# Cross-attention stage of a decoder layer: row factor in the softmax's scale, memory squares from a second load, a buffer per key result, sample scores in half pairs

## The chip, the core and the metric

The kernel runs on one core of a Trainium2 chip. The metric is device time in microseconds (us) of one execution, the median over several runs. The engines are PE (TensorE, matrix products; its weight loads are PEld), ACT (ScalarE), DVE (VectorE), POOL (GpSimd) and SP (SyncE, which here issues most of the transfers between the chip's memory and the core's own).

## The reference

One layer of a hybrid decoder serves a prompt (512 tokens) and a sample group (8 sequences of 8 tokens), 1024 channels, everything in fp32. In order: a half-step SwiGLU block, a mixer (a linear recurrence and trailing means) with an output projection, cross-attention over 256 memory tokens, a second half-step SwiGLU block, a final norm. The part that matters here:

```python
def rmsnorm(x, g):
    var = mean(x * x, axis=-1)
    return x * rsqrt(var + EPS) * g

m = rmsnorm(mem, mem_norm)          # 256 memory tokens of the prompt
k = (m @ wk).reshape(b, 256, 4, 256)
v = (m @ wv).reshape(b, 256, 4, 256)

h = rmsnorm(x, xattn_norm)
q = (h @ wq).reshape(b, t, 4, 256)
s = einsum('bthd,bmhd->bhtm', q, k) * 256 ** -0.5
p = softmax(s, axis=-1)
x = x + einsum('bhtm,bmhd->bthd', p, v).reshape(b, t, 1024) @ wo
```

The prompt uses the keys and values computed here, which are outputs too; each sample sequence uses cached keys and values of its own (`cache_mem_k`, `cache_mem_v`).

## The kernel before

Tokens lie along the free axis: `x` holds 8 chunks of 128 channels by 576 tokens (`T`: 512 prompt tokens `TP` and 64 sample tokens `TS`), in two halves of 288 (`HT`). Precision is kept by splitting every fp32 operand into a high and a low part (`split`: ACT casts to the high part, L191; DVE subtracts for the low part, L194) and multiplying high·high, high·low and low·high, three matmuls for one. Weights come as fp32 panels into a ring of buffers (`wr`) and are split into `wh` and `wl`. Projections over both token halves are done as seven products of half the size (a Strassen scheme): `HalfNorm` keeps, beside the two plain operands, sums and differences of chunks and halves (`sums`, `last`); the weights of a query need such sums too (`prepare_q`, steps h, f, m, g).

The stage that is changed lies at 481 to 645 us. It runs so:

- Out projection `wo`, eight panels j. As each output chunk is done DVE adds it to `x` (L1269), and `nx.add` splits the new chunk and squares it (ACT) and adds the squares into `acc` (DVE, L262). `nx.sums` makes the Strassen sums, two subtractions of each on POOL (L363, L364). Beside this, the RMS of the memory tokens is prepared: `mem_square` squares the eight chunks of the memory (channels as rows), sums them into `macc` (L1251 to L1255), one-column matmuls with `ones` at j == 5 add over the channels (`row_factor`), `spread` turns the factor into a row (L319), and at j == 6 all eight chunks are multiplied by gain and factor (L1282) and split into `mh` and `ml`.
- Memory keys `k`, eight panels of 24 matmuls (`mem_k`). From each PSUM bank ACT casts and DVE subtracts `kk`; ACT also copies it to a buffer `ko` (L1299), one of two, and stores it (`o_k`, ACT's queue). After panel 2 comes `rstd_wide`: the sum of squares of `x`, split in two, is multiplied with a matrix of means (`mw_nx`, L302), and ACT (Ln, Exp) and DVE (L304 to L311) form the factor `r`, spread over all 128 rows.
- Queries p = 0 to 3 (`query`), two heads' halves each: seven products U, B, A, U, C, B, C of twelve matmuls into four banks. The weight sums of a query (`prepare_q`, L1333 to L1339) are on POOL, their splits on ACT and DVE, one query ahead. At its end a query's two results `q1` and `q0` are multiplied by `r` (L1387, L1391), split into `qq`, and the sample tokens are copied into `z` (L1385), in which each sequence has its own columns. `z` is cleared on POOL (L1381) for each query.
- Sample scores `ss`: for each 128 rows of the queries, two key tiles `ck` of 512 KB are loaded (SP, L1307), and 8 matmuls into 32 columns each accumulate. Query p takes steps 2p−2 and 2p−1 together, and their tiles go into the same ring `wr` as the weights.
- Then the memory values `v`, the prompt's scores `s`, the softmax (`softmax`: maximum on DVE, Exp on ACT with a constant scale of 256^−0.5 and the maximum as bias), and the products with the values.

The order of each engine's instructions is made by a scheduler from the program's order and the dependencies; on PE the queries' products keep the program's order by added links. Buffers of a pool with one tag are reused in turn, and a new use waits for the last reader of the old one. Each engine, and each queue of transfers, works strictly in its order.

Of the kernel before, what the change touches and what calls it, by code (L numbers as in the profile page):

```python
# [69 lines left out]
def hybrid_step(ctx, tc, a):  # L70
# [163 lines left out]
    class Norm:  # L234
# [18 lines left out]
        def rstd_wide(self):  # L253
            return row_factor_wide(self.acc, self.name)

# [13 lines left out]
    def row_factor(accs, name, ps, n=T, parts=2):  # L269
# [3 lines left out]
        offs = blocks(n, parts)  # L273
# [18 lines left out]

    def row_factor_wide(acc, name, n=T):

        h = n // 2
        ps = bank(f"mw_{name}")
        r = rows.tile([P, n], F32, tag=f"rstd{n}", bufs=1, name=f"rstd_{name}")
        parts_ = [rows.tile([P, T], F32R, tag="sq", name=f"acc{q}_{name}")[:, :n] for q in "hl"]
        split(*parts_, acc)
        for i in range(2):  # L300
            for k, q in enumerate(parts_):
                te.matmul(ps[:, i, :h], lhsT=mean, rhs=q[:, i * h:(i + 1) * h], start=k == 0, stop=k == 1)  # L302
        u, y = (rows.tile([P, T], F32, tag="sq", name=f"{q}_{name}")[:, :n] for q in ("var", "t"))
        v.tensor_scalar(halves(u), ps[:, :, :h], EPS, None, op0=ALU.add)  # L304
        s.activation(y, u, AF.Ln)
        s.activation(r, y, AF.Exp, scale=-0.5)

        v.tensor_mul(y, r, r)
        v.tensor_mul(y, y, u)
        v.tensor_scalar(y, y, -0.5, 1.5, op0=ALU.mult, op1=ALU.add)  # L310
        v.tensor_mul(r, r, y)  # L311
        return r
# [19 lines left out]
    class HalfNorm(Norm):  # L332
# [17 lines left out]
        def sums(self, p, t, eng=None):  # L350

            eng = eng or v
# [14 lines left out]
        def last(self, i, t, eng=None):  # L367

            self.last_sum(i, t, eng)
            self.last_split(i, t)  # L370
# [5 lines left out]
        def last_sum(self, i, t, eng=None):  # L376
# [6 lines left out]
            (eng or v).tensor_sub(t, t, f(lo[:, :, T2, :]))  # L383
# [856 lines left out]
    if True:  # L1240
# [6 lines left out]
        macc = xp.tile([P, ML], F32, tag="macc", name="macc")  # L1247

        def mem_square(j):
            if j == 0:  # L1250
                s.activation(macc, mem[j], AF.Square)  # L1251
            else:
                sq = rows.tile([P, ML], F32, tag="sq", name="msq")
                s.activation(sq, mem[j], AF.Square)
                v.tensor_add(macc, macc, sq)  # L1255
# [5 lines left out]
        for j in range(DC):  # L1261
            wos.append((bank(f"wo{j}"), panel(a["w_out"][j], DC, P, "o", freed if j else None)))

            project(*wos[j], yy, range(LC, DC), last=False)
            if j < 2:
                continue
            for i in range(3) if j == 2 else (j,):
# [3 lines left out]
                if i in (1, 3, 5):  # L1271
                    nx.sums(i // 2, sums_in(raw_, DC * ML + (i // 2 % 2) * 3 * HT), nc.gpsimd)
            for i in range(3 * j - 6, min(3 * j - 3, DC)):
                mem_square(i)
            background()
            if j == 5:
                mq = row_factor([macc], "mem", wos[j][0][:, 1, :], ML)
            if j == 6:
                mr = spread(mq, "mem", ML)
                mh, ml = (xp.tile([P, DC, ML], F32R, name=f"m{q}") for q in "hl")  # L1280
                for i in range(DC):
                    v.scalar_tensor_tensor(out=mem[i], in0=mem[i], scalar=col("gk", i), in1=mr,  # L1282
                                           op0=ALU.mult, op1=ALU.mult)
                    split(mh[:, i, :], ml[:, i, :], mem[i])
# [60 lines left out]
        def query(p):  # L1345
# [8 lines left out]
            if p == 0:  # L1354
                for i in range(2):
                    t = late[:, (3 + 2 * i) * HT:(5 + 2 * i) * HT].rearrange("p (a n) -> p a n", a=2)
                    nx.last(i, t, nc.gpsimd)
# [356 lines left out]
```

## Time and profile before

| | us |
|---|---|
| median of 3 runs | 1137.74 (1135.87 to 1138.07) |
| profiled execution, its own time | 1137.22 |
| its span | 1135.4 |
| PE busy | 1106.1 (97%) |
| DVE busy | 891.7 (79%) |
| ACT busy | 689.6 (61%) |
| POOL busy | 228.8 (20%) |
| mean granted PE clock | 0.993 |

The span is the time from the first to the last instruction that the profiler shows; the execution's own time is 1.8 us more. A row of a timeline gives start, duration, engine, line, operation, output and inputs, and in brackets the idle time just ahead with what ended it. A group gives the sum of the busy time and the mean in nanoseconds behind the first bar, and the idle time behind the second. A window gives for PE, PEld, DVE, ACT and POOL the busy time and the count, then the granted clock of PE (1.00 is full speed), the share of the transfer engines and GB/s. The line numbers are those of the kernel before; in the changed kernel the same lines stand lower or higher by some tens.

### The profile page before, as it was taken

To read this page: it belongs to the slowest core of one execution; us is meant where nothing else is said; L and a number is where in the kernel's file an instruction comes from. 1 tells how busy PE (TensorE), PEld (TensorE's weight loads), DVE (VectorE), ACT (ScalarE), POOL (GpSimd) and SP (SyncE) were. 2 spreads that over 40 slices of the span, in tenths; PEclk is the share of its full clock that TensorE was granted. 3 is DMA by queue.
4 is the path that set the end of the run, shared out by engine and by line. 5 is a ranking of instruction groups with operands and counts; after the bars stand their busy time and mean duration, and the time that the engine had idled before them with its cause. 6 is when DMAs were issued, how large, how long until landed. Compare 5 with 4: busy or idle time off the path is not lost.

```text
span 1135.4 us, 21982 instructions
## 1 busy us (share of the span) xinstructions
PE 1106.1 (97%) x8382; PEld 1085.0 (96%) x8382; DVE 891.7 (79%) x1574; ACT 689.6 (61%) x1296; POOL 228.8 (20%) x265
## 2 busy tenths in 40 slices
PE   9999999999999999998789999999999999999997
PEld 8999999999999999998778888999999999999996
DVE  7999888879865978889955656779988888787754
ACT  8566666666664645866743445546666666666554
POOL 0012222221221033334342000000222222222210
PEclk9999999999999999999999999999999999999998
DMA  9457777676766655666535973332677876877652
GB/s 309 124 133 174 164 158 168 158 170 143 170 141 138 200 143 136 147 162 140 130 107 200 352 271 104 82 93 72 158 174 166 184 174 154 186 157 167 140 113 84
DMA packets 95259, 180.15 MB, mean 159 GB/s; under 512 B 9969, under 2 KB 47857, under 8 KB 95025
## 3 DMA queue, kind: packets, MB, share of 16 engines
q1 hardware_dynamic: 61024, 124.68, 34.2%
q0 software_dynamic: 31472, 51.65, 27.8%
q10 hardware_dynamic: 2656, 2.41, 0.6%
q8 instruction: 65, 1.06, 0.4%
q14 instruction: 42, 0.34, 0.1%
HBM read 140.87 MB, written 13.20 MB: 136 GB/s over the span
## 4 chain that ended last, share of the span: by engine, by line
PE 46%; issue 1%; DMA 1%; DVE 1%; POOL 1%; ACT 0%; POOLq 0%; SPq 0%; ACTq 0%; DVEq 0%
PE pu L148 12%; PE pc L148 6%; PE dU L148 4%; PE xo L148 4%; PE pd L148 3%; PE pa L148 3%; PE v L1431 2%; PE pg L148 1%; PE o L148 1%; PE dC L148 1%; PE dA L148 1%; PE dD L148 1%; PE s L148 1%; PE qc L148 1%; DMA ck<-ck 1%
## 5 line engine op out<-in xcount | busy, mean ns | idle before, releaser
L475 POOL DMA_DIRECT2D r<-f_gu x39 | 34.7, 890 | 349.9 <-DVE r L472 94.6
L191 ACT CAST dh<-td 128x512 fp32r<-128x512 f32 x96 | 59.3, 618 | 30.8 <-PE dA L148 9.9
L148 PE MATMUL dU<-ph,dh 128*128 128x288 f32 x256 | 75.9, 296 | 1.4 <-ACT add L661 1.4
L148 PE MATMUL dU<-ph,dl 128*128 128x288 f32 x256 | 75.6, 295 | 0.0
L148 PE MATMUL dU<-pl,dh 128*128 128x288 f32 x256 | 75.6, 295 | 0.0
L194 DVE TENSOR_TENSOR dl<-td,dh 128x512 fp32r<-128x512 f32 x96 | 64.6, 685 | 10.1 <-ACT dh L191 10.0
L194 DVE TENSOR_TENSOR wl_e<-r,wh_e 128x1024 fp32r<-128x1024 f32 x39 | 47.7, 1222 | 27.9 <-ACT wh_e L191 27.8
L677 POOL DMA_DIRECT2D x<-add_e x32 | 38.9, 1215 | 141.4 <-ACT add_e L661 46.6
L704 POOL DMA_DIRECT2D x<-add x32 | 30.7, 961 | 139.7 <-ACT add L661 94.0
L191 ACT CAST wh_g<-r 128x1024 fp32r<-128x1024 f32 x39 | 41.0, 1050 | 27.6 <-PE pc L148 13.4
L194 DVE TENSOR_TENSOR wl_h<-r,wh_h 128x1024 fp32r<-128x1024 f32 x39 | 47.6, 1220 | 3.2 <-ACT wh_h L191 3.1
L148 PEld LDWEIGHTS dU<-ph,dh 128*128 128x128 f32 x256 | 48.2, 188 | 1.9 <-ACT add L661 1.9
L148 PEld LDWEIGHTS dU<-ph,dl 128*128 128x128 f32 x256 | 48.3, 188 | 0.0
L148 PEld LDWEIGHTS dU<-pl,dh 128*128 128x128 f32 x256 | 48.2, 188 | 0.0
L194 DVE TENSOR_TENSOR wl_g<-r,wh_g 128x1024 fp32r<-128x1024 f32 x39 | 47.6, 1221 | 0.3 <-ACT wh_g L191 0.3
L191 ACT CAST wh_h<-r 128x1024 fp32r<-128x1024 f32 x39 | 40.9, 1049 | 10.3 <-PE pu L148 7.3
L191 ACT CAST wh_e<-r 128x1024 fp32r<-128x1024 f32 x39 | 41.1, 1055 | 0.6 <-PE pg L148 0.6
L885 ACT ACTIVATE g<-g 128x576 f32<-128x576 f32 x39 | 26.6, 683 | 23.9 <-DVE g L884 22.2
L711 POOL DMA_DIRECT2D x<-add x32 | 36.5, 1142 | 1.0 <-ACT add L661 0.8
L191 ACT CAST ph<-g 128x576 fp32r<-128x576 f32 (+1 forms) x39 | 22.9, 588 | 18.6 <-DVE g L591 10.4
L850 ACT COPY e<-pc 128x288 f32<-128x288 f32 x39 | 15.6, 400 | 29.5 <-PE pc L148 28.6
L661 ACT ACTIVATE add<-dU 128x288 f32<-128x288 f32 x64 | 26.1, 408 | 11.6 <-PE dU L148 11.6
(643 smaller groups left out, 4686.4 us busy)
## 6 DMA issues: line engine op xcount, KB each, us to landing
x<-add POOLq DMA_DIRECT2D x80, 288.0 KB, 5.7
r<-f_gu SPq DMA_DIRECT2D x39, 512.0 KB, 4.0
r<-f_gu SPq DMA_DIRECT2D x78, 256.0 KB, 3.5
td<-f_d SPq DMA_DIRECT2D x80, 128.0 KB, 5.1
r<-f_gu POOLq DMA_DIRECT2D x39, 256.0 KB, 4.6
x<-add_e POOLq DMA_DIRECT2D x32, 288.0 KB, 4.8
dsum<-f_d POOLq DMA_DIRECT2D x32, 256.0 KB, 4.8
ck<-ck SPq DMA_DIRECT2D x16, 512.0 KB, 4.9
```

What stands on the lines that cost most here:

```text
L148: i = te.matmul(*args, **kw)
L191: i = cast[0] = s.copy(hi, src)
L194: return v.tensor_tensor(out=lo, in0=src, in1=f(hi), op=ALU.subtract)
L475: nc.gpsimd.dma_start(r0[:, 0], wgu[f - plain, :, 3], accum_op=ALU.add)
L661: taken[0] = s.activation(dst, src, AF.Copy, scale=0.5 * sign)
L677: nc.gpsimd.dma_start(x[:, j:j + 2, HT:], t, accum_op=ALU.add)
L704: nc.gpsimd.dma_start(x[:, 2 * (i % NQ), :], t, accum_op=ALU.add)
L711: nc.gpsimd.dma_start(x[:, 2 * (i % NQ) + 1, :], t, accum_op=ALU.add)
L850: out_[0] = s.copy(e1, C)
L885: silu = s.activation(g, g, AF.Silu, scale=-1.0)
L1431: te.matmul(ps[:, m, :HD], lhsT=lhs[:, kd, ms], rhs=w[wi][:, k, :], start=kd == 0 and i == 0, stop=kd == DC - 1 and i == 2)
```

## The change

1. The memory's squares: the memory is loaded a second time with tokens as rows (`mem_r`, two tiles of 512 KB), and two ACT squares add up each token's squares as they go (`mem_rows`). The factor follows at j == 2 (`mem_factor`), without matmuls; it is spread at j == 3; two chunks are multiplied and split at each of j = 3 to 6 (`mem_split`).
2. The queries' row factor: `rstd_wide` is gone. Five one-column matmuls and ACT's Sqrt give the factor with tokens as rows. The prompt's part `pr_`, with 256^−0.5 in it, is the scale of the softmax's Exp; the sample's part is spread by one 128×128 matmul (`rs`) and multiplied in where the sample tokens go to `z`.
3. The subtractions of `sums` and `last_sum`, the weight sums of query 0 and the addition of a query's U to q1 move from POOL to DVE. The weight sums h and m of query 0 are made at key panels 5 and 6, the loads of query weights are issued a panel or more earlier.
4. The copy of each key panel has a place of its own in the tile `late`.
5. There are two `z`, cleared ahead of the queries and again by POOL for p > 1. The sample scores are done one step at a time, two places in a query, in the order 1, 0, 3, 2, 5, 4, 7, 6, and the key tiles of a step are loaded ahead.
6. An Exp on a small tile in query 1.

The diff, cut to its core:

```diff
-    def row_factor_wide(acc, name, n=T):
...
@@ HalfNorm.sums (last_sum alike)
-            eng.tensor_sub(t2, b22, t1)
-            eng.tensor_sub(t3, b12, b22)
+            v.tensor_sub(t2, b22, t1)
+            v.tensor_sub(t3, b12, b22)
@@ memory
-        def mem_square(j):
...
+        def mem_rows():
+            for i in range(2):
+                q = wp.tile([P, DC * P], F32, tag="wr", bufs=WRB, name=f"mr{i}")
+                nc.sync.dma_start(q, a["mem_r"][i])
+                s.activation(q, q, AF.Square, accum_out=mss[:, i:i + 1])
+
+        def mem_factor():
+            u, y, q = (rows.tile([P, 8], F32, tag=f"rf{i}", bufs=1, name=f"rf{i}_mem")[:, :2] for i in range(3))
+            s.activation(y, mss, AF.Sqrt, bias=eps, scale=1.0 / (DC * P))
+            v.tensor_scalar(u, mss, 1.0 / (DC * P), EPS, op0=ALU.mult, op1=ALU.add)
+            rsqrt(q, u, y)
+            return q
+
+        def mem_split(i):
+            v.scalar_tensor_tensor(out=mem[i], in0=mem[i], scalar=col("gk", i), in1=mr, op0=ALU.mult, op1=ALU.mult)
+            split(mh[:, i, :], ml[:, i, :], mem[i])
@@ out projection
+            if j == 1:
+                mem_rows()
...
-            if j == 5:
-                mq = row_factor([macc], "mem", wos[j][0][:, 1, :], ML)
-            if j == 6:
+            if j == 2:
+                mq = mem_factor()
+            if j == 3:
                 mr = spread(mq, "mem", ML)
...
+            if 2 < j < 7:
+                for i in (2 * j - 6, 2 * j - 5):
+                    mem_split(i)
@@ mem_k
-            o = (xp if j % 2 else rows).tile([P, ML], F32, tag="macc" if j % 2 else f"rstd{ML}", bufs=1, name=f"ko{j}")
+            o = late[:, 7 * HT + j * ML:7 * HT + (j + 1) * ML]
@@ sample scores
+        def load_keys(j, tags=("wr", "wr")):
...
+            for g, q in enumerate(cks[j]):
+                nc.sync.dma_start(q, a["ck"][g, j])
+
+        def sample_scores(j):
...
+                    mm(sps[b * 32:(b + 1) * 32, g, :ML], lhsT=zz[p % 2][:, 4 * g + b, e, :],
+                       rhs=q[:, b, :], start=j == 1, stop=j == DC - 2)
@@ prepare_q
-            g = nc.gpsimd
+            g = nc.gpsimd if p else v
@@ query
+                v.tensor_mul(z[:, :, e, p * ST:(p + 1) * ST], q[:, TP:].rearrange("p (b k) -> p b k", k=ST),
+                             rs.rearrange("p (b k) -> p b k", k=ST))
+            load_q(p + 2)
...
+            else:
+                sample_scores(2 * p - 1)
+                load_keys(2 * p - 2)
             prepare_q(p + 1, "h")
...
-            nc.gpsimd.tensor_add(q1[:, HT:], q1[:, HT:], q0[:, HT:])
+            v.tensor_add(q1[:, HT:], q1[:, HT:], q0[:, HT:])
...
+            if p:
+                sample_scores(2 * p - 2)
+            if p < KP - 1:
+                load_keys(2 * p + 1)
...
-            v.tensor_mul(q1, q1, r)
...
+            if p == 1:
+                s.activation(nr[:, :1], ones, AF.Exp)
@@ after each key panel
             if j == 2:
-                r = nx.rstd_wide()
+                q = row_factor([nx.acc], "nx", ps[:, 1, :], offs=[0, P, 2 * P, 3 * P, T - P])
+            if j == 3:
+                te.matmul(ps[:, 1, :P], lhsT=q[:, 4:5].to_broadcast([P, P]), rhs=ident, start=True, stop=True)
+                s.copy(rs, ps[:, 1, P - TS:P])
+                v.tensor_scalar(pr_, q[:, :4], HD ** -0.5, None, op0=ALU.mult)
+            if j in (2, 4):
+                load_q(j // 2 - 1)
+            if j == 5:
+                prepare_q(0, "h")
+            if j == 6:
+                prepare_q(0, "m")
+        prepare_q(0, "f")
+        prepare_q(0, "g")
@@ softmax
-                s.activation(pt[:, i, :], ps[:, i, :], AF.Exp, bias=mx[:, i:i + 1], scale=HD ** -0.5,
+                s.activation(pt[:, i, :], ps[:, i, :], AF.Exp, bias=mx[:, i:i + 1],
+                             scale=HD ** -0.5 if r is None else r[:, i:i + 1], accum_out=sm[:, i:i + 1])
```

The table of orders at three places. First ACT from the copy of key panel 5 to the first copy of a query product; `wh_qF` and `wh_qG` are casts of query 0's weight sums, `ko` or `t_nx` the copy of a panel's keys. Before:

```order
L1299 COPY ko5_6983<-k5_6956 128x256
L191 CAST kk_6746<-k6_6996 128x256
L1300 DMA o_k<-ko5_6983 128x256
L191 CAST wh_qF_7077<-q0_0_6910 128x1024
L1299 COPY ko6_7023<-k6_6996 128x256
L1300 DMA o_k<-ko6_7023 128x256
L191 CAST kk_6746<-k7_7032 128x256
L1299 COPY ko7_7059<-k7_7032 128x256
L191 CAST wh_qG_7082<-q0_0_6910 128x512
L1300 DMA o_k<-ko7_7059 128x256
L1351 COPY q0_7099<-qu0_7095 128x288
```

and now:

```order
L1283 COPY t_nx_6719<-k5_6938 128x256
L191 CAST kk_6728<-k6_6978 128x256
L1284 DMA o_k<-t_nx_6719 128x256
L191 CAST wh_qF_7048<-q0_0_6851 128x1024
L1283 COPY t_nx_6719<-k6_6978 128x256
L1284 DMA o_k<-t_nx_6719 128x256
L191 CAST kk_6728<-k7_7017 128x256
L191 CAST wh_qG_7053<-q0_0_6851 128x512
L1283 COPY t_nx_6719<-k7_7017 128x256
L1284 DMA o_k<-t_nx_6719 128x256
L1345 COPY q0_7073<-qu0_7069 128x288
```

The cast wh_qF stands ahead of panel 6's copy in both; the sum that it casts is made on POOL before, on DVE now.

Second, DVE around the end of the out projection, where `L1282` (now L1240) multiplies the memory's chunks and `ml` is their low part. Before:

```order
L194 TENSOR_TENSOR nxl_6148<-mem,nxh_6147 128x864
L1269 TENSOR_TENSOR x<-wo_6582,x 128x576
L194 TENSOR_TENSOR wl_k<-wr_k,wh_k 128x1024
L196 SCALAR_TENSOR_TENSOR nxl_6148<-x,neg,nxh_6147 128x576
L262 TENSOR_TENSOR acc_nx<-acc_nx,sq 128x576
L1282 SCALAR_TENSOR_TENSOR mem<-mem,cst,rstd_mem 128x256 x3
L194 TENSOR_TENSOR ml<-mem,mh 128x256 x3
```

and now:

```order
L337 SCALAR_TENSOR_TENSOR mem<-x,neg,b_nx_6422 128x288
L339 TENSOR_TENSOR mem<-b_nx_6422 128x288
L338 TENSOR_TENSOR mem<-b_nx_6422,mem 128x288
L1240 SCALAR_TENSOR_TENSOR mem<-mem,cst,rstd_mem 128x256 x3
L194 TENSOR_TENSOR nxl_6146<-mem,nxh_6145 128x864
L194 TENSOR_TENSOR ml<-mem,mh 128x256 x2
L1257 TENSOR_TENSOR x<-wo_6443,x 128x576
```

The first three chunks of the memory now stand ahead of the addition of the fifth output chunk, not behind that of the seventh, and the two subtractions of the sums stand on DVE beside them.

Third, SP's queue from the weights of query 2 on; `wqs` are query weights, `ck` the key tiles, whose second digit is the step. Before:

```order
L1322 DMA q0_2_7062<-wqs 128x1024
L1322 DMA q1_2_7063<-wqs 128x1024
L1322 DMA q0_3_7234<-wqs 128x1024
L1322 DMA q1_3_7235<-wqs 128x1024
L1307 DMA ck00_7334<-ck 128x1024
L1307 DMA ck10_7335<-ck 128x1024
L1307 DMA ck01_7346<-ck 128x1024
L1307 DMA ck11_7347<-ck 128x1024
```

and now:

```order
L1309 DMA q0_2_7075<-wqs 128x1024
L1309 DMA q1_2_7076<-wqs 128x1024
L1293 DMA ck01_7175<-ck 128x1024
L1293 DMA ck11_7176<-ck 128x1024
L1309 DMA q0_3_7219<-wqs 128x1024
L1309 DMA q1_3_7220<-wqs 128x1024
L1293 DMA ck00_7257<-ck 128x1024
L1293 DMA ck10_7258<-ck 128x1024
```

The tiles of step 1 now stand ahead of query 3's weights, all later ones behind them, one step after the other.

More of the change, by code (lines that the diff above doesn't have):

```diff
@@ L291, in rsqrt @@
         return v.scalar_tensor_tensor(out=q, in0=y, scalar=1.5, in1=q, op0=ALU.add, op1=ALU.mult)
-    def row_factor_wide(acc, name, n=T):
[L295 to L312, printed above, removed]
     def spread(q, name, n=T):
@@ L1409, in hybrid_step @@
         qq = []
-        z = rows.tile([P, T], F32, tag="acc", bufs=1, name="z")[:, :2 * NB * 4 * ST].rearrange(
-            "p (b e k) -> p b e k", b=NB, e=2)
+        zz = [rows.tile([P, T], F32, tag=tag, bufs=1, name=f"z_{tag}")[:, :2 * NB * 4 * ST].rearrange(
+            "p (b e k) -> p b e k", b=NB, e=2) for tag in ("acc", f"rstd{T}")]
+        for z in zz:
+            nc.gpsimd.memset(z, 0.0)
         pinned[0], chain[0] = True, latest[0]
@@ L1526, in out @@
             project(*wos[j], qq, ks, hs, first, last)
+        for j in (DC - 1, DC - 2):
+            load_keys(j, tags=("wh", "wl"))
         mem_v(0)()
[L1529 removed]
+        for j in (DC - 1, DC - 2):
+            sample_scores(j)
         at = now["r1"].tile([P, DC * T], F32, tag="A", bufs=2, name="at")
@@ L1630, in _inputs @@
     out["memT"] = chunks(i["mem_prompt"][0])
+    out["mem_r"] = i["mem_prompt"][0].reshape(2, P, DC * P)
     inv = np.broadcast_to(1.0 / np.arange(1, PW + 1, dtype=np.float32), (P, PW))
```

95 lines of the change are left out of this document (36 added, 59 removed).

## The prediction

> **What bounds the kernel now.** I read the page's top first, to learn which engine is the bound and where it isn't busy.
>
> ```profile
> PE 1106.1 (97%) x8382; PEld 1085.0 (96%) x8382; DVE 891.7 (79%) x1574; ACT 689.6 (61%) x1296; POOL 228.8 (20%) x265
> PE   9999999999999999998789999999999999999997
> ```
>
> PE is busy nearly throughout. A slice is 28.4 us, and the only ones under nine tenths lie at 511 to 596 us: the end of the out projection, the memory keys, and the first one and a half of the four queries. All that the change edits lies there, so what it can win is PE's idle and slow time in that stretch. The view of PE's waits from 480 to 800 us lists the idle time with its releasers (sum, times, longest).
>
> ```profile
> PE qu L148 <- ACT ko L1299: 4.6, 1, 4.6
> PE ss L148 <- DMA ck<-ck: 3.8, 2, 3.2
> PE wo L148 <- DVE x L1269: 2.0, 1, 2.0
> PE qu L148 <- ACT q L1351: 1.4, 1, 1.4
> PE k L148 <- DVE ml L194: 1.0, 1, 1.0
> PE k L148 <- ACT ko L1299: 1.0, 1, 1.0
> PE qc L148 <- DVE q L1374: 0.9, 1, 0.9
> PE k L148 <- DVE wl_k L194: 0.3, 1, 0.3
> ```
>
> Together 15.0 us. The windows of 2 us add what no wait shows, the granted clock (third number from the right).
>
> ```profile
> 568.00:570.00 2.00, 2.00 (x10) 2.00 (x10) 0.45 (x2) 0.86 (x2) 1.28 (x1) 0.50 0.17 57
> 584.00:586.00 2.00, 0.63 (x5) 0.40 (x5) 1.93 (x4) 0.90 (x3) 0.00 (x0) 1.00 0.68 252
> 598.00:600.00 2.00, 2.00 (x13) 1.35 (x6) 0.20 (x1) 0.00 (x0) 0.52 (x1) 0.50 0.93 352
> ```
>
> After the two long waits PE runs at half clock for some 3 us; after the wait of 1.4 at 584 it doesn't. A long wait is therefore paid one and a half times.
>
> **The largest wait, term 1.** PE, POOL and ACT by their timelines around it (start, duration, and in brackets the idle time before):
>
> ```profile
> 562.26 0.28 PE L148 MATMUL k<-mh,wl_k 128*128 128x256 f32 x1
> 567.10 0.61 PE L148 MATMUL qu<-nxh,wh_qH 128*128 128x288 f32 x1 [4.56 <-ACT ko L1299]
> 570.15 0.33 PE L148 MATMUL qb<-nxh,wh_qH 128*128 128x288 f32 x1
> 563.58 2.12 POOL L1334 TENSOR_TENSOR q<-q 128x512 f32<-128x512 f32 x1
> 565.73 1.04 ACT L191 CAST wh_qF<-q 128x1024 fp32r<-128x1024 f32 x1 [2.62 <-POOL q L1334]
> 566.68 0.36 ACT L1299 COPY ko<-k 128x256 f32<-128x256 f32 x1
> ```
>
> The first query product takes over a bank of the memory keys, which the copy L1299 of key panel 6 must have read. On ACT that copy stands behind the cast wh_qF, which waits for POOL's subtraction L1334. In the changed order the sums L1333/L1334 of query 0 are on DVE, and the product's bank is one that the row factor's small matmuls used last; the copies have a place of their own for each panel (no wait for an earlier panel's store). The chain POOL, wh_qF, ko, qu no longer exists. Removed: 4.56, and the half clock: 570.15 − 567.10 = 3.05 for the product's twelve matmuls, against 1.58 for an undisturbed one (qu x12 below), 1.47. **6.0 us.**
>
> **Term 2, the sample scores of query 1.** PE's timeline, then the chain of waits for an undisturbed group and for the transfers:
>
> ```profile
> 592.16 1.07 PE L148 MATMUL ss<-ck,z 128*32 128x256 f32 x16
> 596.39 0.64 PE L148 MATMUL ss<-ck,z 128*32 128x256 f32 x8 [3.16 <-DMA ck<-ck]
> 598.66 0.61 PE L148 MATMUL qc<-nxh,wh_qG 128*128 128x288 f32 x1
> 601.36 0.29 PE L148 MATMUL qu<-nxh,wh_qH 128*128 128x288 f32 x1
> 611.04 1.86 PE ss L148 x32
> 612.90 1.79 PE qc L148 x12
> 614.70 1.58 PE qu L148 x12
> 593.29 4.31 DMA ck<-ck
> 628.17 6.77 DMA ck<-ck
> ```
>
> From 592.16 to 601.36 the scores and the product behind them took 9.20 us; undisturbed 1.86 + 1.79 = 3.65. The second pair of key tiles was late because its buffers came free only when the first had been used. Now each pair is loaded a step ahead and used apart from its neighbour. Removed: **5.5 us.** Only the pair of step 3 is tight: its load starts when pair 0's scores end, and it is due three products and a pair's scores later, some 3 × 1.6 = 4.8 plus small gaps, 5.2 us. A landing took 4.3 here (the page's median is 4.9, the longest I found 6.8), so at the median it isn't late, at the longest by 1.6.
>
> The price: four more switches between scores and products. The product behind a group takes 1.79 instead of 1.58, so 4 × 0.21 = **0.8 us added**, in any case.
>
> **Term 3, query 0's own stalls.** DVE's timeline:
>
> ```profile
> 578.69 0.46 DVE L1374 TENSOR_TENSOR q<-qc,q 128x288 f32<-128x288 f32 x1 [4.19 <-POOL q L1370]
> ```
>
> DVE stood 4.19 us for the addition L1370, which stood on POOL behind three of query 0's and query 1's weight sums, with everything for query 1 behind it on DVE. That addition is DVE's own now. Removed are the waits on q L1374 and q L1351: 0.9 + 1.4 = **2.3 us.** POOL's weight sums for queries 1 to 3 stay, one query ahead.
>
> **Term 4, the out projection and keys.** The wait for x L1269 belongs to the one-column matmuls on macc, which must follow a DVE read of their bank:
>
> ```profile
> 523.04 0.61 PE L148 MATMUL wo<-ones,macc 128*128 128x1 f32 x4 [1.96 <-DVE x L1269]
> 523.50 0.52 PE L148 MATMUL wo<-yl,wh_o 128*128 128x288 f32 x2
> ```
>
> Matmuls and wait go: 1.96 + 0.46 = 2.4. The memory's products and splits, until now one block ahead of the first key panel, are spread over four steps, so ml is ready: 1.0. With copies of their own the wait for ko goes: 1.0; the wl_k wait: 0.3. **4.7 us removed.** The two extra loads (512 KB each) and their two squares on ACT replace eight squares; nothing on PE waits for them unless the row factor, due a step later, is late.
>
> **Term 5, the new row factor.** The wide factor's four matmuls go (0.13 apart, 0.5); five one-column products come, two records each at 0.46/4 = 0.115, 1.15, and one 128×128, 0.2. **0.8 us added.** The Ln/Exp work leaves ACT and DVE (the groups, busy time and mean ns behind the bar):
>
> ```profile
> L308 DVE TENSOR_TENSOR t_nx<-rstd_nx 128x576 f32<-128x576 f32 x1 | 1.2, 1164 | 1.6 <-ACT rstd_nx L306 1.6
> L305 ACT ACT_TABLE_LOAD x1 | 1.3, 1283 | 0.4 <-ACT ko L1299 0.4
> ```
>
> L308 is the longest of six DVE operations of the wide factor, the others 0.45 to 0.76, 4.6 in all. The two multiplications of every query by it go too; the prompt's factor now rides in the Exp at no instruction, the sample's in the copy to z that was there anyway. ACT needs an Exp table once more before the softmax: the preload meant for query 1 stands far ahead in ACT's order, before the row factor's Sqrt. The cover:
>
> ```profile
> 639.50 0.48 ACT L1445 ACTIVATE at<-ss,mxs 128x256 f32<-128x256 f32 x1 [2.16 <-DVE mxs L1443]
> ```
>
> ACT is idle 2.16 us ahead of the first Exp. I book 0; uncovered it would be one load, 1.28 by the row of L305. The Trainium skill, "ScalarE: Activation LUTs", section "What ACT_TABLE_LOAD costs", has the same 1283 ns and adds a drain of about 1380 ns: by it a switch is 2.66 us and up to 0.5 would show, an estimate; this trace shows no drain.
>
> **Term 6, DVE as the next bound.** What POOL and the row factor gave up, DVE must do:
>
> ```profile
> 500.00:520.00 20.00, 20.00 (x153) 20.00 (x152) 16.79 (x22) 13.85 (x24) 10.31 (x11) 1.00 0.71 161
> 520.00:535.00 15.00, 13.04 (x100) 12.81 (x99) 13.84 (x27) 10.06 (x17) 4.30 (x5) 1.00 0.65 159
> 535.00:550.00 15.00, 12.96 (x105) 12.53 (x105) 14.85 (x24) 10.85 (x20) 5.79 (x5) 1.00 0.51 116
> 550.00:567.00 17.00, 12.28 (x101) 11.86 (x99) 14.59 (x19) 11.86 (x19) 7.74 (x5) 0.99 0.39 115
> ```
>
> And two of the groups, up to 535 us:
>
> ```profile
> L1255 DVE TENSOR_TENSOR macc<-macc,msq 128x256 f32<-128x256 f32 x7 | 4.0, 566 | 0.3
> L1282 DVE SCALAR_TENSOR_TENSOR mem<-mem,cst,rstd_mem 128x256 f32<-128x256 f32 x4 | 1.8, 480 | 0.0
> ```
>
> DVE (fifth number) has 30.6 of 35 us to 535, then 29.4 of 32. To 535 come the rest of the memory block, four more of L1282 at 0.48 or over and five splits at some 0.42 to 0.6, about 5, and six 128×288 subtractions at 0.46 (L1374's row), 2.8; the macc additions go, 4.0: 34.4, while PE, without its wait, leaves 32.6. From there to the queries the 5 and the wide factor's 4.6 go; two 128×288 and two 128×576 subtractions (0.46 and 0.75), four weight sums of 128×512 at 0.7 and five one-column operations at 0.16 come, 6.0: 25.8, and 1.8 pushed on, 27.6, against some 25 of PE's keys. But wl_q, the last nx split and wl_qF, over 4 us in that count, aren't due until two to four products into query 0. So DVE can just keep up or cost up to 2.6; I take 1.5, nearer the upper end since the second matmul on acc also waits for DVE (through the second key panel's copy). **1.5 us added.**
>
> **The sum.** 6.0 + 5.5 + 2.3 + 4.7 = 18.5 removed; 0.8 + 0.8 + 1.5 = 3.1 added; net 15.4. The profiled execution took 1137.2: 1121.8. The median before is 0.5 above it, so **1122 us.**
>
> On the clock: the Trainium skill, "TensorE: Matmul & The Clock Gate", section "Part 1: The HAM clock gate (the "warmup" mystery)", says that an idle window of about 3.4 us halves the clock and that a busy one of that length restores it. The trace agrees in kind: half clock after 4.56 and after the two ck waits of 3.8 together, none after 0.9 to 2.0. By the page two ramps cost 1.7 each, 3.4 instead of the 2.3 that the rows give, and the sum would be 1121, an estimate.
>
> **Rivals.**
>
> *DVE takes the wait over (22%).* The first query product waits about as before, now for wl_qH or nx rather than ko. For it: the balance of term 6 is already over. Against it: the work in excess is due later. If 4.6 and the slow clock behind it (1.4) come back: 1128; with query 0's stalls too, 1130.
>
> *Key pairs late (13%).* Pair 3, or others, land at 6.8 rather than 4.8: 1.6 late each; two of them 3 us, 1125; together over 3 us in one wait with half clock, 1127. For it: the 6.77 row; against it: 4.31 in this very stretch.
>
> *SP's queue blocks, slower (5%).* The loads of query 3's weights stand in SP's queue ahead of all later key pairs, and wait until POOL and DVE have used up two buffers. Held up there, pair after pair would start late. If a landing, counted from the release of its buffer, took over 8.4 us (the 5.2 that pair 3 has and the 3.2 after which the clock halved), six pairs would each cost 3.2 and 2.70 − 1.58 = 1.1 of slow clock: 26 us, 1148. The longest landing found is 6.8, and that of pair 3 alone is so tight, so the chance is small.
>
> *No change (3%)*: other waits replace all, for instance the first two rivals together with k panels starved of wl_k.
>
> *More than forecast (5%)*: term 6 costs nothing and later stages gain from DVE's lighter queries: under 1117.
>
> **How the numbers follow.** The forecast (52%) by itself covers 1117 to 1126: term 6 from 0 to 2.6, one pair late by 1.6, the table load 1.3. The range reaches over the first two rivals, to 1130, and down to 1116; outside remain the slow rival, no change and a little of the rest. A difference of 0.2%, 2.3 us, can just be told from none: faster 0.91, same 0.03, slower 0.06.
>
> **What would show it.** Right: in the profile after, no wait of a query product on ko; the one-column matmul on macc gone; granted clock 1.00 from 555 to 600; each group of scores some 0.9 long with no wait on ck; four table loads where three were. Wrong: a wait of 3 us or more with a releaser on DVE ahead of qu (first rival), ck waits (second), SP's q3 loads issued after pair 3 is due (third). The stretch from the first key panel to the first query product tells term 6: 25 us, or nearer to 28.

## The result

| | median us | runs | ratio to before (95% interval) |
|---|---|---|---|
| before (the three runs above and one more) | 1137.47 | 4 | |
| changed | 1118.22 (1117.78 to 1121.79) | 4 | 0.984 (0.9817 to 0.9863) |
| changed, a second time, beside the last experiments | 1120.89 (1120.30 to 1122.72) | 4 | 0.986 (0.9840 to 0.9879) |

The forecast was 1122 (1116 to 1130). The profiled execution took 1118.5 with a span of 1116.6. Its page's top, and PE's waits from 480 to 800 us:

```profile
PE 1102.0 (99%) x8386; PEld 1082.6 (97%) x8386; DVE 881.7 (79%) x1577; ACT 689.0 (62%) x1293; POOL 212.0 (19%) x247
PE   9999999999999999999999999999999999999997
```

```profile
PE ss L148 <- DMA ck<-ck: 0.9, 2, 0.5
PE o L148 <- ACT pp L191: 0.2, 1, 0.2
```

Of eight waits with 15.0 us one is left, on key tiles. The granted clock is full there, by windows of 20 us (third number from the right):

```profile
540.00:560.00 20.00, 20.00 (x168) 20.00 (x167) 15.52 (x29) 14.17 (x27) 2.42 (x2) 1.00 0.51 157
560.00:580.00 20.00, 19.11 (x159) 17.26 (x158) 14.11 (x21) 8.33 (x13) 8.92 (x7) 1.00 0.43 141
580.00:600.00 20.00, 20.00 (x174) 17.77 (x173) 12.37 (x20) 8.53 (x14) 5.60 (x6) 1.00 0.75 256
```

To place the gain I use the first matmul of each part in PE's timeline. Of the changed kernel:

```profile
479.50 0.42 PE L148 MATMUL wo<-yh,wh_o 128*128 128x288 f32 x2
531.22 0.28 PE L148 MATMUL k<-mh,wh_k 128*128 128x256 f32 x1
555.49 0.29 PE L148 MATMUL qu<-nxh,wh_qH 128*128 128x288 f32 x1
668.97 0.40 PE L148 MATMUL xo<-qh,wh_x 128*128 128x288 f32 x1
```

and of the kernel before:

```profile
481.43 0.43 PE L148 MATMUL wo<-yh,wh_o 128*128 128x288 f32 x2
535.75 0.29 PE L148 MATMUL k<-mh,wh_k 128*128 128x256 f32 x1
687.68 0.40 PE L148 MATMUL xo<-qh,wh_x 128*128 128x288 f32 x1
```

(its qu at 567.10 stands in the prediction). `xo` is the attention's own output projection, the first thing that the change doesn't touch. So the out projection went from 54.32 to 51.72, the keys from 31.35 to 24.27, queries to `xo` from 120.58 to 113.48: the stage from 206.25 to 189.47, 16.8 less. In the second profile of the changed kernel it is 190.88, 15.4 less; the sum of the prediction was 15.4. The remaining 1.9 of the 18.8 between the two spans is in the start of `wo`. That lies between 478.9 and 481.4 in all fourteen profiles, with 481.28 in the changed kernel's second one: variation of the execution. For the experiments I therefore give the stage beside the median; it is one profile each, and two of the same kernel differed by 0.7 and 1.4. Runs of one job are made side by side on one chip, and the jobs ran on different chips; a ratio is to the kernel before in the same job.

### The profile page after: what moved, and what is told of

Its sections match the earlier page's. It is cut to its first block, busy times and chain, and to the rows that moved or that the text cites. A ratio compares the mean times of both kernels' runs of the same rounds, so it can differ in the third digit from the quotient of the medians.

```text
span 1116.6 us, 21977 instructions
## 1 busy us (share of the span) xinstructions
PE 1102.0 (99%) x8386; PEld 1082.6 (97%) x8386; DVE 881.7 (79%) x1577; ACT 689.0 (62%) x1293; POOL 212.0 (19%) x247
## 3 DMA queue, kind: packets, MB, share of 16 engines
q8 instruction: 65, 1.06, 0.4%
## 4 chain that ended last, share of the span: by engine, by line
PE 91%; DMA 3%; DVE 3%; issue 2%; ACT 1%; POOL 0%; POOLq 0%; SPq 0%; DVEq 0%; ACTq 0%
PE pu L148 22%; PE pc L148 10%; PE dU L148 8%; PE pd L148 6%; PE pa L148 5%; PE xo L148 5%; PE wo L148 5%; PE pg L148 4%; PE in_l L148 2%; PE in_p L148 2%; PE in_g L148 2%; PE k L148 2%; PE v L1438 2%; PE dA L148 2%; PE dC L148 2%; PE dD L148 2%
## 5 line engine op out<-in xcount | busy, mean ns | idle before, releaser
L191 ACT CAST dh<-td 128x512 fp32r<-128x512 f32 x96 | 59.3, 618 | 30.8 <-PE dA L148 10.7
```

The costliest lines, as they stand in the source:

```text
L191: i = cast[0] = s.copy(hi, src)
```

## The experiments

| kernel | out projection | keys | queries to xo | stage | median us | ratio to before |
|---|---|---|---|---|---|---|
| before | 54.3 | 31.4 | 120.6 | 206.3 | 1137.47 | |
| before + sums on DVE | 53.5 | 28.4 | 123.8 | 205.6 | 1136.37 | 1.0001 (0.9988 to 1.0013) |
| before + copies of their own | 54.1 | 30.5 | 121.3 | 205.9 | 1136.61 | 0.9996 (0.9982 to 1.0010) |
| before + memory's part | 51.7 | 33.3 | 119.9 | 204.9 | 1135.99 | 0.9985 (0.9971 to 0.9999) |
| changed | 51.7 | 24.3 | 113.5 | 189.5 | 1118.22 | 0.984 |
| changed, second time | 51.7 | 25.0 | 114.1 | 190.9 | 1120.89 | 0.986 |
| − key pairs apart | 51.7 | 24.1 | 121.6 | 197.4 | 1125.26 | 0.9901 (0.9882 to 0.9921) |
| − memory's part | 52.2 | 28.4 | 114.8 | 195.3 | 1124.74 | 0.9898 (0.9883 to 0.9912) |
| − early weights | 51.7 | 27.6 | 115.3 | 194.6 | 1124.47 | 0.9887 (0.9869 to 0.9905) |
| − narrow row factor | 51.7 | 24.6 | 115.1 | 191.3 | 1120.49 | 0.9845 (0.9831 to 0.9860) |
| − sums on DVE | 51.7 | 25.0 | 114.4 | 191.1 | 1119.97 | 0.9841 (0.9825 to 0.9858) |
| + 6.0 us of DVE work in the keys | 51.7 | 28.4 | 114.1 | 194.3 | 1123.76 | 0.9876 (0.9861 to 0.9891) |
| + keys ahead of query 3's weights | 51.7 | 24.3 | 112.3 | 188.3 | 1118.13 | 0.9825 (0.9810 to 0.9839) |
| the same, second time | 51.7 | 24.3 | 113.0 | 189.0 | 1117.82 | 0.983 (0.9811 to 0.9848) |

### One part alone, in the kernel before

**Query 0's weight sums on DVE.**

```diff
-            g = nc.gpsimd
+            g = nc.gpsimd if p else v
```

> The kernel before with one edit: the weight sums of query 0 on DVE instead of POOL. Theory (the chain POOL sum, cast wh_qF, copy ko, first query product is the cause of the 4.6 us and of the half clock behind it): both go, 6.0 us, and POOL's addition in query 0 comes earlier, so 1 to 2.3 more: 1129 to 1131.5. Rival (the shared ko buffers, by their stores, hold the copy): the wait on ko stays at 3 us or more, 1135 or over. Rival (DVE takes the wait over): a wait of 3 us with a releaser on DVE, 1134 to 1137.

No gain that can be measured. Its waits:

```profile
PE ss L148 <- DMA ck<-ck: 3.6, 3, 3.2
PE qc L148 <- DVE q L1374: 2.9, 1, 2.9
PE qu L148 <- ACT ko L1299: 1.9, 1, 1.9
```

The wait ahead of the first query product fell from 4.6 to 1.9, so POOL's sums were a link of the chain; but the keys' gain of 3.0 came back in the queries, 3.2. Four rows say how, PE's timeline, a window, and the timelines of ACT and POOL:

```profile
561.74 0.40 PE L148 MATMUL qu<-nxh,wh_qH 128*128 128x288 f32 x1 [1.94 <-ACT ko L1299]
562.00:564.00 2.00, 2.00 (x10) 2.00 (x10) 2.00 (x4) 1.32 (x2) 0.00 (x0) 0.52 0.20 66
561.32 0.37 ACT L1299 COPY ko<-k 128x256 f32<-128x256 f32 x1 [0.95 <-DMA o_k<-ko]
570.80 1.28 POOL L1339 TENSOR_TENSOR q<-q 128x512 f32<-128x512 f32 x1 [16.49 <-DMA q<-wqs]
```

The shorter wait still halved the clock (0.52). What held the copy at the end was now its shared buffer: it waited 0.95 for an earlier panel's store. And POOL stood 16.5 us for a load: this L1339 is the first sum of query 3, whose weights are loaded last, and in POOL's order it stands ahead of query 1's sums and of the addition L1370, for which DVE and then PE wait 2.9.

**Copies of their own for the keys.**

```diff
-            o = (xp if j % 2 else rows).tile([P, ML], F32, tag="macc" if j % 2 else f"rstd{ML}", bufs=1, name=f"ko{j}")
+            o = late[:, 7 * HT + j * ML:7 * HT + (j + 1) * ML]
```

> The kernel before with one edit: every key panel's copy has a place of its own, as in the changed kernel. Theory: the copy of panel 6 still stands behind the cast that waits for POOL, so the 4.6 us stay; only the wait of 1.0 on ko among the keys goes: 1136 to 1137. Rival (the shared buffers are the cause): 4.6 and the slow clock go, 1131.

As the theory said: the wait ahead of the first query product is 4.2, so the shared buffers alone were not its cause (the run before this one shows them as the next link; no run has both edits alone in the kernel before). But the 1.0 among the keys didn't go either, with ACT's row ahead of that copy:

```profile
PE qu L148 <- ACT t_nx L1299: 4.2, 1, 4.2
PE k L148 <- ACT t_nx L1299: 1.0, 1, 1.0
543.56 0.91 ACT L191 CAST nxh<-t_nx 128x864 fp32r<-128x864 f32 x1 [0.53 <-POOL t_nx L363]
```

ACT's copy stands behind a cast that waited for POOL's subtraction L363, so a buffer of its own doesn't help it.

**The memory's part.** The diff of this part as above, with the wide row factor, POOL's sums and all else as before.

> The kernel before with the memory's part alone (second load with tokens as rows, squares on ACT, factor without matmuls, products and splits spread over panels 3 to 6); the rest as before. New theory (the wait of 4.6 begins with DVE: its split wl_qH, which POOL's sum must follow, is late because the memory's block and the macc additions fill DVE ahead of the keys): the waits of 2.0 and 1.0 go, and with some 5 us less on DVE in the keys the first query product waits at most 2 us and without half clock; query 0's waits on q stay or grow by 1 to 3: 1128 to 1131. Rival (the prediction's theory: the chain begins on POOL and only its move to DVE or the copies mend it): 2.4 and 1.0 are won, the 4.6 stay, 1133.5 to 1134.5.

Neither time came true: 1.3 us less in the stage. The out projection is 2.6 shorter, as foreseen, and the waits for ml and ko in the keys are gone, but the keys are 2.0 longer:

```profile
PE qu L148 <- ACT ko L1308: 4.3, 1, 4.3
PE ss L148 <- DMA ck<-ck: 3.9, 2, 3.3
PE mw_nx L302 <- DVE accl_nx L194: 2.1, 1, 2.1
PE mw_nx L302 <- ACT acch_nx L191: 1.5, 1, 1.5
```

PE now came to the wide factor's matmuls before ACT and DVE had split their operand, and waited there instead, with half clock behind it (0.50 from 544 to 546). ACT was late there because a cast ahead had waited 2.90 for POOL's subtraction L363. And the 4.3 stayed, as the rival had it. Its chain starts on DVE, with the split wl_qH of query 0's first weights, which the sum over the same buffer must follow (POOL L1333 in the kernel before starts at 562.23). That split in the kernel before, here, and in the changed kernel:

```profile
560.88 1.22 DVE L194 TENSOR_TENSOR wl_qH<-q,wh_qH 128x1024 fp32r<-128x1024 f32 x1
```

```profile
555.96 1.22 DVE L194 TENSOR_TENSOR wl_qH<-q,wh_qH 128x1024 fp32r<-128x1024 f32 x1
```

```profile
541.91 1.22 DVE L194 TENSOR_TENSOR wl_qH<-q,wh_qH 128x1024 fp32r<-128x1024 f32 x1
```

Counted from the first key matmul it stands at 25.1 before, at 25.4 here (k at 530.59) and at 10.7 in the changed kernel, where it is issued at panel 5. The weights had long landed: POOL's first sum over them, L1339, ran at 508.75 in the kernel before. So it isn't their load that is late, and what the memory's part leaves of room on DVE doesn't move the split here; what the undo runs below show to move it is its place in the program, and in part the rest of DVE's row.

### One part taken out of the changed kernel

**Early weights.**

```diff
-            if j in (2, 4):
-                load_q(j // 2 - 1)
-            if j == 5:
-                prepare_q(0, "h")
-            if j == 6:
-                prepare_q(0, "m")
-        prepare_q(0, "f")
-        prepare_q(0, "g")
+            if j > 2 and j % 2:
+                load_q((j - 3) // 2)
+        for q in "hmfg":
+            prepare_q(0, q)
```

(with query 2's load behind panel 7 instead of in query 0).

> The changed kernel with the weights of queries 0 to 2 loaded where the kernel before loads them (behind key panels 3, 5 and 7), and query 0's sums and splits all behind panel 7; the weights of query 3 as in the changed kernel. Theory (the early weights are what lets DVE split wl_qH 13 us ahead of its use): wl_qH, and wh_qF behind DVE's sums, fall due at the end of the keys again, and the first query product waits 2 to 4 us, some of it with half clock, 3 to 7 slower, 1121 to 1125. Rival (DVE's room alone decides, the weights were early enough): within 1 of the changed kernel.

The theory holds, 5.1 in the stage against the first profile of the changed kernel and 3.7 against the second; in the same job the medians differ by 3.6. The split wl_qH comes at 550.04, 18.2 behind the first key matmul: later than the 10.7 of the early place, earlier than the 25 of the kernel before, with the other parts in. A wait for a key copy is back, with half clock (0.50 from 560 to 562):

```profile
PE qu L148 <- ACT t_nx L1283: 2.4, 1, 2.4
558.46 0.62 ACT L191 CAST wh_qG<-q 128x512 fp32r<-128x512 f32 x1 [0.97 <-DVE q L1323]
```

It is the prediction's chain with other members: a weight sum, now on DVE (L1323), the cast behind it, the copy of the last key panel behind that (558.98), and the product (559.40). This run has the sums on DVE and a place for each copy, and still waits.

**The memory's part.**

```diff
-            if j == 1:
-                mem_rows()
...
+            for i in range(3 * j - 6, min(3 * j - 3, DC)):
+                mem_square(i)
...
+            if j == 5:
+                mq = row_factor([macc], "mem", wos[j][0][:, 1, :], ML)
+            if j == 6:
                 mr = spread(mq, "mem", ML)
...
+                for i in range(DC):
                     mem_split(i)
```

> The changed kernel with the memory's part undone: eight ACT squares summed into macc, one-column matmuls at panel 5, all eight products and splits at panel 6, no second load. Theory: the wait of the one-column matmul (2.0), its 0.46 and the wait for ml (1.0) come back, and DVE has 4.0 of additions more in a stretch where it has no room: 3.5 to 5 slower, 1121.5 to 1123. Rival (the waits belonged to POOL's sums, which held DVE then): 0.5 to 1 slower, 1119.

Slower by 5.9 in the stage against the first profile of the changed kernel, more than either said, by 4.5 against the second, and not where they said: there is no wait for macc, the out projection is only 0.4 longer. The loss stands in the keys, 4.1:

```profile
PE qu L148 <- ACT t_nx L1277: 2.6, 1, 2.6
558.16 0.37 ACT L1277 COPY t_nx<-k 128x256 f32<-128x256 f32 x1 [1.91 <-DVE kk L194]
```

Here the split wl_qH is early (545.84), but DVE, with the memory's block ahead of the keys, comes late to the low part kk of panel 6, and ACT's copy of that panel stands behind it. The copy that PE waits for, the last panel's at 560.05, follows on ACT without a pause. So there are two ways to a wait for a key copy: the weights' chain and DVE's whole row.

**Room on DVE.**

```diff
+            if 0 < j < 5:
+                for i in range(2):
+                    v.tensor_mul(xtemp(T, f"extra{j}{i}"), x[:, 0, :], x[:, 1, :])
```

> The changed kernel with eight multiplications of 128x576 more on DVE (0.75 each, 6.0 us in all), two behind each of key panels 1 to 4; their result is not used. It measures DVE's room in the keys. Theory (the balance of the prediction was too strict; DVE was busy 22.0 of the 24.3 us of the keys, and part of that isn't due yet): 2.3 us of room and some 2 of work that can wait, so 1 to 3 slower, 1119 to 1121. Rival (DVE just keeps up, as the prediction had it): nearly all of it shows, 5 to 8 slower with the clock, 1123 to 1126.

Nearer the rival: of 6.0 us 4.8 show in the stage against the first profile (4.2 in the keys), 3.4 against the second, and the wait is again one for the last panel's copy:

```profile
PE qu L148 <- ACT t_nx L1283: 2.7, 1, 2.7
PE k L148 <- DVE wl_k L194: 0.7, 1, 0.7
```

So the changed kernel has 1.2 us of room on DVE by one profile and 2.6 by the other, about what DVE is idle in the keys (22.0 busy of 24.3 us). The theory's further 2 us of work that can wait did not show. In the changed kernel's second profile PE already waited 0.5 for a copy in the keys.

**Narrow row factor.** Back are the wide factor, the multiplication of each query's results by it and the constant scale of the Exp; one z, cleared by halves, since the second one's place is taken by the factor; the Exp of change 6 is out.

```diff
-                q = row_factor([nx.acc], "nx", ps[:, 1, :], offs=[0, P, 2 * P, 3 * P, T - P])
+                r = row_factor_wide(nx.acc, "nx")
...
+            v.tensor_mul(q1, q1, r)
             finish(1, q1)
...
+            v.tensor_mul(q0, q0, r)
             finish(0, q0)
```

> The changed kernel with the wide row factor again (four matmuls with the matrix of means, Ln and Exp, factor multiplied into both results of each query on DVE); one z, cleared by halves on POOL. Theory (DVE has room enough, the factor itself is not on the path): PE saves 0.8, the multiplications hide: within 1.5 of the changed kernel, 1117 to 1119.5. Rival (DVE is next in line and these 4.6 and 6.9 us are what made room): a wait on DVE of 2 us or more at the first query product or between queries, 1121 to 1125.

1.8 slower in the stage against the first profile, 0.4 against the second. Nearer the theory: no wait of 2 us, but several small ones that the changed kernel hasn't, 0.8 on wl_k, 0.6 on a copy of q, 0.4 on z and 0.6 ahead of a score group. What the title puts first is worth 0.4 to 1.8 us once the rest is there.

**Sums on POOL.**

```diff
-            g = nc.gpsimd if p else v
+            g = nc.gpsimd
...
-            v.tensor_add(q1[:, HT:], q1[:, HT:], q0[:, HT:])
+            nc.gpsimd.tensor_add(q1[:, HT:], q1[:, HT:], q0[:, HT:])
```

> The changed kernel with the weight sums of query 0 and the additions of U to q1 on POOL again. Theory: the first query product no longer hangs on a copy behind wh_qF, but its fourth (F) needs the cast itself, and DVE's row in query 0 hangs on POOL again: 1 to 5 slower, 1119 to 1123, with waits on wl_qF or q in query 0. Rival (what mattered is only the order on ACT and the ko buffers): same time.

1.6 slower against the first profile of the changed kernel, 0.2 against the second, and no wait on any sum:

```profile
PE ss L148 <- DMA ck<-ck: 1.5, 2, 1.0
PE k L1399 <- DVE rf_nx L288: 0.2, 1, 0.2
```

With wl_qH at 541.80 POOL has the time, and query 3's first sum now stands behind query 1's sums and the addition, not ahead of them:

```profile
563.98 0.80 POOL L1368 TENSOR_TENSOR q<-q,q 128x288 f32<-128x288 f32 x1
573.01 1.40 POOL L1326 TENSOR_TENSOR q<-q 128x512 f32<-128x512 f32 x1 [4.96 <-DMA q<-wqs]
```

Which engine adds the weights hardly matters here; when it may start does. The subtractions of `sums` stay on DVE in this run: no run tests their move apart, though ACT waited for them on POOL in two runs above (0.53 and 2.90).

**Key pairs apart.**

```diff
-                sample_scores(2 * p - 1)
-                load_keys(2 * p - 2)
...
-                sample_scores(2 * p - 2)
-            if p < KP - 1:
-                load_keys(2 * p + 1)
+                for j in (2 * p - 2, 2 * p - 1):
+                    load_keys(j)
+                    sample_scores(j)
```

(alike for the last two steps behind the first values).

> The changed kernel with the sample scores of two steps together again, in the order 0 to 7, each step's tiles loaded where they are used (two z stay). Theory: the first group of query 1 waits for its tiles as before, 3 to 4 us, with half clock behind it; the 0.9 that the changed kernel waits on tiles and two or three switches at 0.2 go: 3.5 to 4.5 slower, 1121.5 to 1123. Rival (with query 0 no longer stalled the tiles come at another time and are hidden anyway): within 1 of the changed kernel, 1117 to 1119.

About twice what was expected: 8.0 in the stage against the first profile, 6.6 against the second.

```profile
PE ss L148 <- DMA ck<-ck: 3.8, 2, 3.2
PE qu L148 <- ACT q L1345: 1.8, 1, 1.8
PE t L1476 <- DVE at L1456: 0.8, 1, 0.8
```

The 3.8 on tiles are back, with half clock behind them. Two more waits come. The 1.8 is in query 1: without a step's scores between, PE reaches the second product into U's bank before ACT has copied the first (at 571.01, behind a cast of query 0's result); half clock follows. It stands where the kernel before has its 1.4 on q L1351, and it is here although the addition of U is on DVE. The 0.8 stands behind the table load: with both last score groups behind the values, ACT loads the Exp table at 627.98, and the softmax ends too late for the transposes `t`. The kernel before, with the same order but no load there, has no such wait. In the changed kernel PE doesn't wait for the load:

```profile
618.57 1.28 ACT L1455 ACT_TABLE_LOAD   x1 [2.66 <-DVE mxs L1451]
```

It stands behind ACT's idle time, not in it, since it too begins only when the maximum is there. The Exp of change 6 doesn't help: ACT runs it, with a table load of its own at 500.79, ahead of the row factor's Sqrt (load at 543.88).

### One more change of order

**Keys ahead of query 3's weights.**

```diff
-            load_q(p + 2)
+            if p == 0:
+                load_q(2)
...
                 load_keys(2 * p - 2)
+                load_q(p + 2)
```

> The changed kernel with the two loads of query 3's weights put behind those of key step 0 in SP's queue (both in query 1); nothing else. Theory (the only wait left, 0.9 us on the tiles of step 0, comes from sharing the transfer engines with these 1 MB, which nobody needs for another 20 us): the wait goes, 0.5 to 1.1 faster than the changed kernel, 1117.2 to 1117.7. Rival (the tiles' buffers come free too late whatever the order): same time, the wait of 0.9 stays.

> The changed kernel itself, to compare with keys_first on the same chip: 1118 to 1119.

> The changed kernel with query 3's weights behind key step 0 in SP's queue, again, beside the changed kernel. Theory: the 0.9 of waits on tiles are worth 0.5 to 1.1: 1117 to 1118, and 0.5 to 1.1 below the changed kernel in this job. Rival (the profiled gain is given back or is below what the times tell): within 0.3 of it.

In the changed kernel the tiles of step 0 are issued behind 1 MB of weights and land late:

```profile
571.38 7.57 DMA ck<-ck
577.85 0.64 PE L148 MATMUL ss<-ck,z_acc 128*32 128x256 f32 x8 [0.39 <-DMA ck<-ck]
```

With the order turned round the waits on tiles are gone in the first profile and 0.5 in the second, where the changed kernel beside it has 1.5; the 0.5 is on step 3, the one that the prediction held to be tight. In that job it took 1117.82 (1116.85 to 1118.74) against 1120.89 (1120.30 to 1122.72): the ranges don't touch. The changed kernel was above the 1118 to 1119 expected of it, and the difference of 3.1 is more than the 0.5 to 1.1 expected. The stage accounts for 1.9 of the 3.1, the start of `wo` (480.17 against 481.28) for 1.1, which the edit doesn't touch. In the earlier job it took 1118.13, without the changed kernel beside it, no less than the changed kernel's own first 1118.22. By the stage, two profiles of each, it is 1.6 us faster in the mean (188.6 against 190.2); that it is faster rests on one job and these profiles.

## Why the prediction was right, and where its steps were not

- **The bound and the sum** held. All the waits named went and the clock stayed full; 15.4 was forecast, 16.8 and 15.4 were measured in the stage. The median of the first job is 3.8 below the forecast, that of the second 1.1. Of the signs named one failed: the score groups still wait on ck. That the sum fits so well is in part luck: the waits of terms 1 and 3 went by other edits than those named, and term 6 added 1.5 that wasn't there.
- **Term 1** (6.0) had the right size, but its levers don't do it. The chain POOL, wh_qF, ko, qu was there, but the prediction began it at POOL's subtraction. It begins at DVE's wl_qH, issued behind the last key panel. Moving the sums to DVE leaves 1.9 and half clock; moving them back costs 0.2 to 1.6; giving each copy its place does nothing alone. With both, but without the early issue, 2.4 and half clock remain, 3.7 to 5.1 in the stage, in a chain of the same kind: that it "no longer exists" was wrong. The change listed it, the load and sums at panels 2 to 6, and the prediction passed over it.
- **Term 2** (5.5, and 0.8 for switches): the waits and the half clock went, and taking it out cost 6.6 to 8.0, with two waits more than the term has. Step 3 was held to be tight; it was step 0 that was late, by 0.9 and 1.5, behind query 3's weights. That is the place of the slow rival, SP's queue, with one step late instead of six, 0.9 to 1.5 us instead of 26, and without half clock.
- **Term 3** (2.3): gone, but not because the addition L1370 left POOL; with it on POOL again query 0 has no such wait. The prediction took the sum at the head of POOL's row for one of query 0 or 1. It was query 3's, waiting for its load, and that now stands behind. The 1.4 on q L1351 went by term 2's edit: with whole pairs it is back as 1.8, with the addition on DVE.
- **Term 4** (4.7): the out projection gave 2.6 for a forecast of 2.4, and ml and ko went. That it could be counted alone was wrong: alone, the wait moved to the wide factor's matmuls, 2.1 + 1.5 and half clock.
- **Term 5** (0.8 added) can't be told apart in the times. The table load costs PE nothing, as booked, but for another reason: it isn't covered by ACT's idle time, it follows it, and the first Exp comes 1.28 later without PE waiting. The run with whole pairs shows that this is tight.
- **Term 6** (1.5 added) is the mis-sized one: 0 in the first profile, 0.5 in the second (ahead of the matmuls on acc, where it was looked for). To the first key matmul DVE was reckoned to 34.4 us of work where 32.6 were to be had; by windows from the same matmul on it was busy

```profile
498.07:531.22 33.15, 33.15 (x251) 33.15 (x250) 31.23 (x53) 22.39 (x38) 9.15 (x10) 1.00 0.77 188
531.22:555.49 24.27, 24.27 (x207) 24.27 (x206) 21.99 (x38) 18.14 (x32) 3.50 (x3) 1.00 0.54 153
```

  31.2, and in the keys 22.0 instead of 27.6. The durations of the kernel before were too long for it, since many of DVE's operations had run beside POOL's (below). Each compared with the same operation standing alone in the same trace, they are 3.1 us too long from 500 to 535 and 5.1 in the keys, in the changed kernel 0.0 and 0.3 (estimates); that is nearly all of the 3.2 and 5.6 by which the balance was too high. But the direction was right: with 6.0 us more DVE is the bound, as in the first rival, though the wait is 2.7 and without half clock.

What the terms hide is that they don't add. Alone in the kernel before, three parts gave 0.6, 0.3 and 1.3 in the stage; the memory's part, 1.3 alone, costs 5.9 when it is taken out of the changed kernel (4.5 by its second profile). Each wait had another close behind it. Not tested apart are the subtractions of `sums` on DVE and, in the changed kernel, the copies' own places, the second z and the Exp of change 6.

## What to carry to other kernels

A wait's releaser is the last link; follow the row on that engine back to the first instruction that was late, and ask whether it was late for want of room or because it was issued late. Here the first was a split on DVE that stood behind eight panels of other work, and where it stood in the program was worth more than which engine did the next step. When several waits end within a few microseconds of each other, a part tried alone shows little or nothing, and an undo in the finished kernel shows what it holds up.

## What the hardware showed that I had not expected

**The clock doesn't go by the length of the wait alone.** A wait of 1.94 us ahead of the first query product (sums on DVE alone, rows above) was followed by a granted clock of 0.52, one of 1.81 (key pairs apart taken out) by 0.50 from 572 to 574. One of 2.7 us with DVE's extra work was not, by the windows around it (PE starts at 559.79):

```profile
558.00:560.00 2.00, 0.21 (x1) 0.21 (x2) 2.00 (x5) 0.94 (x2) 0.00 (x0) 1.00 0.02 5
560.00:562.00 2.00, 2.00 (x16) 2.00 (x16) 1.98 (x4) 0.94 (x2) 0.00 (x0) 1.00 0.48 90
```

The prediction took the border to lie between 2.0 and 3.2. The Trainium skill, "TensorE: Matmul & The Clock Gate", section "Part 1: The HAM clock gate (the "warmup" mystery)", says that the window runs freely, which would let the same wait fall well or badly; that half clock needs a whole window of about 3.4 us idle isn't what these runs show.

**Some of DVE's operations are longer beside POOL's.** The same subtraction with a scalar on 128×288, before (with POOL's two subtractions beside it) and changed (with them on DVE):

```profile
L362 DVE SCALAR_TENSOR_TENSOR mem<-x,neg,b_nx 128x288 f32<-128x288 f32 x3 | 2.6, 879 | 0.0
```

```profile
L337 DVE SCALAR_TENSOR_TENSOR mem<-x,neg,b_nx 128x288 f32<-128x288 f32 x3 | 1.5, 512 | 0.0
```

The 879 is a mean of unlike ones. The first of the three, with POOL idle, took 0.51; the other two took twice that. DVE's and POOL's timelines of the kernel before:

```profile
502.45 0.51 DVE L362 SCALAR_TENSOR_TENSOR mem<-x,neg,b_nx 128x288 f32<-128x288 f32 x1
513.45 1.06 DVE L362 SCALAR_TENSOR_TENSOR mem<-x,neg,b_nx 128x288 f32<-128x288 f32 x1
513.31 0.88 POOL L364 TENSOR_TENSOR mem<-b_nx 128x288 f32<-128x288 f32 x1 [1.71 <-ACT b_nx L361]
```

It ended some 0.3 us behind POOL's operation, and so did the two others of this line that met one (at 525.43 and 543.76): it looks as if DVE waited for POOL rather than ran slower. The split wl_q of query 0 takes 2.23 before and 1.22 now. But the split kk, with one operand in PSUM, took 0.41 at 564.50 although POOL was busy. So work that moves from POOL to DVE can cost DVE less than its length, since what stood beside it gets shorter. The Trainium skill, "GPSIMD Engine Reference", section "1. Specifications", says that POOL shares its SBUF interfaces with DVE; the rows agree, 1.06 against 0.51 us.
